# A hybrid MLA and NSA decoder block: a reordered first stage, and q's inverse norm as a factor of the score rows

## The chip, the cores and the metric

The kernel runs on one core of a Trainium2 chip. The metric is the device time of one execution in microseconds, as the median of several runs. PE is the matrix engine, with its weight loads counted apart as PEld; DVE is the vector engine, ACT the scalar engine, POOL the GpSimd engine, and SP the engine whose queue issues nearly all DMAs. [...]

## The reference: what is computed

One decoder block for a sequence of 512 rows of width 1024, in float32. Cut to what matters:

```python
mod = silu(c) @ ada_w + ada_b                       # c: one row; ada_w: 1024 x 6144
sh1, sc1, gt1, sh2, sc2, gt2 = split(mod, 6)
h = rms_norm(x, norm1_gain) * (1 + sc1) + sh1
z = h @ w_in                                        # all projections of both mixers
y_mla = mla_attention(...) @ w_o_mla                # 8 heads, q and k of 96 = 64 + 32 rotary
y_nsa = nsa_attention(...) @ w_o_nsa                # 8 heads of 64: compressed, selected, window
x = x + gt1 * ((sigmoid(g_mla) * y_mla + sigmoid(g_nsa) * y_nsa) @ w_out)
h2 = rms_norm(x, norm2_gain) * (1 + sc2) + sh2
x = x + gt2 * ((silu(h2 @ ffn_w_gate) * (h2 @ ffn_w_up)) @ ffn_w_down)
```

In both mixers q is normed and turned before the scores: `q = rope(rms_norm(q, q_gain))`, `s = q @ k.T * scale`, `p = softmax(s + mask)`. The inverse norm of q is one number for each row and head. Since a rotation keeps a factor of the row, and the score of a row is linear in q, that number may be multiplied in before the product or into the row of scores behind it.

## The kernel before

Tiles have 128 partitions. The 512 rows of x are four tiles (`NT` = 4), the width 1024 is eight slabs (`KD` = 8). Each float32 operand of a large product is split into a high and a low part (`whi` and `wlo` for weights, `hTh` and `hTl` for h), and a product is three matmuls: high by high, low by high, high by low. ACT makes the high part of a weight slab, DVE or POOL the low part. PSUM tiles come from three pools: `mm` with four buffers, `sc` with two, `tp` with two.

**The first stage** (0 to about 70 us) makes h transposed and the first wide product with w_in. `gemm_wide` goes through the eight slabs k; for each, `make_h(k)` needs two columns of the modulation: `mod_column(k)` loads strips of ada_w 128 columns wide (tile `araw`, four row blocks in a DMA, four DMAs for each k), multiplies each row block by its silu(c) with ACT and DVE and adds them up (tile `acc`), two of the blocks added by POOL. For k = 0 some blocks go to PE directly. `mod_sum` adds over the partitions with PE (tile `pm`), then DVE adds the bias and makes `modc`. With `modc`, h of slab k is scaled (`h`, `hTh`, `hTl`), and PE makes 24 matmuls into `wa` and 24 into `wb`. The low parts of these weights are POOL's (`eng_lo=pool`). The 22 small loads (gains, positions, masks, `small_loads`, L502 to L526) are written behind this stage; SP's queue takes them between the strips.

**Preparation of NSA** (to about 170 us): q of NSA (`UQ`) gets its inverse norm `rsq`, gain and rotation; keys (`kd`) and compressed keys follow. **NSA** (170 to 339 us): for each of eight units the scores of a head come out of PE into `pw` and `ps`; DVE adds the mask and takes the row minimum in one instruction (`tensor_tensor_reduce`; scores are negated; the trace calls it CUSTOM_DVE_ANT_0), ACT takes the exponential.

**MLA** (339 to about 575 us): `gemm_tok` makes q in two groups of four heads (`gq`); `use_q` copies it to `qn` (ACT), sums squares (DVE, `msq` from the squares `jq`), applies the rotary gain `g_q` and the rotation (POOL). `norm_q(c)` makes the inverse norm of group c by a chain of small DVE instructions on 128x16 (`rq_i_q`, `rq_h_q`, `rq_m_q`, ending in `rsq`), and multiplies each of the four `qn` by it. `mla_heads` transposes q and k of one head (PE, `pt`) and splits them (`qh`, `ql`, `kh`, `kl`); `mla_scores` makes the scores (`ps`, pool `sc`) and minima; `mla_values` the weighted sum. Between the heads' steps PE is given work from elsewhere: the merge gates (`gp`), and columns of the modulation for later stages (`mods`, DVE's `macc` from strips `raw` of ada_w). `as_filler(norm_q(1))` lays the second group's norm over the steps of head 0, with a quota of 5 steps.

The rest (575 to 914 us) is the merge, w_out and the feed-forward network.

Every instruction is issued through a helper that records it, so all stand at L144 in the trace; DMA issues have their own lines (L253 for weights, L401 for `araw`, L913 for the strips of `mods`). Instructions of an engine run in the order of its queue. A scheduler sets that order from the code and its own estimate of times, so a change also moves instructions elsewhere. Of the DMAs that SP issues a limited number is under way at a time: an issue waits for the landing of an earlier one.

## Time and profile before

| | us |
|---|---|
| median of 3 runs | 918.6 |
| lowest and highest | 915.64, 920.27 |
| the profiled execution | 915.57 |
| its span in the trace | 913.6 |
| PE busy | 850.4 |
| DVE busy | 645.8 |
| ACT busy | 435.6 |
| POOL busy | 202.3 |

The span is the time from the first to the last instruction of the profiled execution; its own time is 2 us longer. The busy time of an engine is an average over stages with different limits, so the rows further down go by stage: how much PE works in a stretch and at what granted clock, and on what it waits. In a timeline row the brackets at the end say how long the engine had been idle and which operation released it.

### The profile page before, as it was taken

To read this page: it belongs to the slowest core of one execution; us is meant where nothing else is said; L and a number is where in the kernel's file an instruction comes from. 1 tells how busy PE (TensorE), PEld (TensorE's weight loads), DVE (VectorE), ACT (ScalarE), POOL (GpSimd) and SP (SyncE) were. 2 spreads that over 40 slices of the span, in tenths; PEclk is the share of its full clock that TensorE was granted. 3 is DMA by queue.
4 is the path that set the end of the run, shared out by engine and by line. 5 is a ranking of instruction groups with operands and counts; after the bars stand their busy time and mean duration, and the time that the engine had idled before them with its cause. 6 is when DMAs were issued, how large, how long until landed. Compare 5 with 4: busy or idle time off the path is not lost.

```text
span 913.6 us, 13079 instructions
## 1 busy us (share of the span) xinstructions
PE 850.4 (93%) x4644; PEld 727.6 (80%) x4644; DVE 645.8 (71%) x1310; ACT 435.6 (48%) x872; POOL 202.3 (22%) x256
## 2 busy tenths in 40 slices
PE   4799999899999996699998989999999999999997
PEld 3689889777787795588776869787899889988986
DVE  6977876778975788557868898866565566455644
ACT  5445655787764733276645344442344224432440
POOL 2422316534332047131228014000000000000000
PEclk9899999999999998699999999999999999999999
DMA  9944545221100743224478770643233413333312
GB/s 306 273 129 121 147 129 146 81 70 53 42 13 35 230 140 114 81 70 157 167 237 304 215 224 25 206 139 97 65 104 115 125 50 104 104 117 91 93 47 92
DMA packets 101732, 115.47 MB, mean 126 GB/s; under 512 B 6036, under 2 KB 74244, under 8 KB 101668
## 3 DMA queue, kind: packets, MB, share of 16 engines
q1 hardware_dynamic: 101508, 114.48, 40.9%
q8 instruction: 36, 0.59, 0.3%
q14 instruction: 28, 0.23, 0.1%
q0 software_dynamic: 64, 0.13, 0.0%
q10 hardware_dynamic: 96, 0.03, 0.0%
HBM read 106.24 MB, written 8.39 MB: 125 GB/s over the span
## 4 chain that ended last, share of the span: by engine, by line
PE 69%; DVE 14%; DMA 9%; issue 3%; ACT 3%; POOL 2%; SPq 1%; DVEq 0%; ACTq 0%; POOLq 0%
PE d L144 13%; PE fu L144 12%; PE gp L144 10%; PE fx L144 6%; PE ga L144 5%; PE fy L144 4%; DMA raw<-in_ada_w_dram 4%; PE pt L144 4%; PE av L144 3%; DMA araw<-in_ada_w_dram 3%; DVE wlo L144 3%; DVE macc L144 2%; PE ps L144 2%; PE wa L144 2%; PE fg L144 2%
## 5 line engine op out<-in xcount | busy, mean ns | idle before, releaser
L144 ACT ACTIVATE whi<-raw 128x1024 fp32r<-128x1024 f32 (+4 forms) x162 | 142.5, 893 | 174.9 <-PE d L144 58.8
L144 DVE TENSOR_TENSOR wlo<-raw,whi 128x1024 fp32r<-128x1024 f32 (+3 forms) x114 | 135.1, 1187 | 71.8 <-ACT whi L144 71.5
L144 POOL TENSOR_TENSOR wlo<-raw,whi 128x512 fp32r<-128x512 f32 (+1 forms) x48 | 66.8, 1410 | 63.5 <-ACT whi L144 59.7
L144 PE MATMUL fu<-h2l,whi 128*128 128x512 f32 (+1 forms) x192 | 71.2, 372 | 0.0
L144 PE MATMUL fu<-h2h,whi 128*128 128x512 f32 (+1 forms) x192 | 70.7, 372 | 0.0
L144 PE MATMUL fu<-h2h,wlo 128*128 128x512 f32 (+1 forms) x192 | 69.9, 373 | 0.0
L144 PE MATMUL d<-whi,mh 128*128 128x512 f32 x176 | 69.8, 398 | 0.0
L144 PE MATMUL d<-wlo,mh 128*128 128x512 f32 x176 | 69.6, 395 | 0.0
L144 PE MATMUL d<-whi,ml 128*128 128x512 f32 x176 | 67.0, 394 | 0.0
L144 ACT ACTIVATE s<-s,mn 128x384 f32<-128x384 f32 (+3 forms) x96 | 52.4, 547 | 27.1 <-DVE mn L144 26.5
L144 DVE TENSOR_TENSOR plo<-pt,phi 128x512 fp32r<-128x512 f32 (+2 forms) x78 | 46.3, 602 | 24.0 <-ACT phi L144 23.6
L144 PE MATMUL gp<-hTh,whi 128*128 128x512 f32 x128 | 55.2, 431 | 0.8 <-ACT qn L144 0.8
L144 ACT ACTIVATE phi<-pt 128x512 fp32r<-128x512 f32 (+2 forms) x78 | 40.1, 526 | 32.0 <-PE pt L144 31.2
L144 PE MATMUL gp<-hTh,wlo 128*128 128x512 f32 x128 | 51.5, 402 | 0.0
L144 PE MATMUL gp<-hTl,whi 128*128 128x512 f32 x128 | 51.3, 401 | 0.0
L144 DVE SCALAR_TENSOR_TENSOR macc<-raw,csil,macc 128x512 f32<-128x512 f32 x45 | 37.2, 832 | 8.1 <-DMA raw<-in_ada_w_dram 7.6
L144 PEld LDWEIGHTS fu<-h2l,whi 128*128 128x128 f32 x192 | 36.2, 188 | 6.1
L144 PEld LDWEIGHTS fu<-h2h,whi 128*128 128x128 f32 x192 | 35.9, 189 | 6.0
L144 PEld LDWEIGHTS fu<-h2h,wlo 128*128 128x128 f32 x192 | 35.6, 189 | 5.6
L144 PEld LDWEIGHTS d<-whi,mh 128*128 128x128 f32 x176 | 33.0, 188 | 8.3 <-issue 0.2
L144 PEld LDWEIGHTS d<-whi,ml 128*128 128x128 f32 x176 | 33.0, 188 | 8.1
L144 PEld LDWEIGHTS d<-wlo,mh 128*128 128x128 f32 x176 | 33.0, 188 | 7.9 <-issue 0.2
(431 smaller groups left out, 2455.3 us busy)
## 6 DMA issues: line engine op xcount, KB each, us to landing
raw<-in_ada_w_dram SPq DMA_DIRECT2D x26, 512.0 KB, 4.5
raw<-in_ffn_w_gate_dram SPq DMA_DIRECT2D x22, 512.0 KB, 3.7
raw<-in_ffn_w_up_dram SPq DMA_DIRECT2D x22, 512.0 KB, 3.8
raw<-in_ffn_w_down_dram SPq DMA_DIRECT2D x22, 512.0 KB, 4.7
araw<-in_ada_w_dram SPq DMA_DIRECT2D x32, 256.0 KB, 5.1
raw<-in_w_in_dram SPq DMA_DIRECT2D x16, 512.0 KB, 3.7
spill<-gs SPq DMA_DIRECT2D x24, 256.0 KB, 2.0
raw<-in_w_in_dram SPq DMA_DIRECT2D x12, 352.0 KB, 3.5
```

What stands on the lines that cost most here:

```text
L144: out = call(*args, **kw)
```

## The change

1. **First stage.** Columns k = 2, 3 and 4, 5 are made in pairs (`PAIRED`) from strips 256 columns wide; the bytes and the number of DMAs stay, each row piece is 1 KB long, not 512 B. Column 0 goes to PE with all its eight blocks, column 1 with four. Of the other columns ACT makes the first block and DVE adds seven; POOL adds nothing. The low parts of w_in in this stage are DVE's.
2. **Small loads.** All 22 are ordered on SP's queue behind the last strip (`late_load`, `follow_dma`).
3. **The row factor.** The multiplications of q by its inverse norm go: four of `UQ` in NSA, eight of `qn` in MLA. The factor becomes the scale of the minima (`scale=rs`, `scale=rsq[...]`) and of the compressed scores. `norm_q` gives one step to its filler quota (1, not 5). The gain `g_q` goes into the rotation tables once (`c2q`, `snq`), and POOL's eight multiplies of `qn` by it go.
4. **Smaller edits.** `kd` is made in one instruction, not two; the rotation of `kpr` in 4 instructions, not 16; the loads of w2 move from POOL's queue to SP's; a DMA scratch area is made smaller.

```diff
-    def mod_column(k):
+    def mod_columns(k, nk, direct):
...
+            raw = ada_strip(r0, nr, k, nk)
...
-                if k == 0 and r < DIRECT:
+                if r < direct:
                     terms.append((src, s))
-                    continue
...
+                elif acc is None:
+                    acc = sp0.tile([P, w], F32, name=f"acc{k}", tag="acc", bufs=2)
                     act.activation(out=acc, in_=src, func=AF.Copy, scale=s)
-                    if r == 1:
-                        pool.tensor_tensor(out=accs[0], in0=accs[0], in1=acc, op=ALU.add)
...
     def make_h(k):
-        pm, terms = mod_column(k)
+        if k not in PAIRED:
+            sums = k, 1, *mod_columns(k, 1, (KD, KD // 2)[k] if k < 2 else 0)
+        elif k % 2 == 0:
+            sums = k, 2, *mod_columns(k, 2, 0)
+        else:
+            sums = None
...
+    def late_load(**kw):
+        follow_dma(sp.dma_start(**kw).ins, ada_last[0])
...
-            sp.dma_start(out=posi[:, t : t + 1], ...)
+            late_load(out=posi[:, t : t + 1], ...)
...
-    run(gemm_wide(hA, w_in, KD, SEG_B, 512, 256, use_q, use_c, hook=make_h, eng_lo=pool))
+    run(gemm_wide(hA, w_in, KD, SEG_B, 512, 256, use_q, use_c, hook=make_h))
...
-            dve.tensor_tensor(out=u, in0=u, in1=rs[:, t, :].unsqueeze(2).broadcast_to([P, 8, 64]), op=ALU.mult)
...
-            for j in range(2):
-                dve.tensor_tensor(out=kd[:, :, j, :], ...)
+            dve.tensor_tensor(out=kd, in0=u.unsqueeze(2).broadcast_to([P, 4, 2, 64]), ...)
...
+            rs = rs_n[:, t, h : h + 1]
-            dve.tensor_tensor(out=cm[:, r, :], ..., op=ALU.add)
+            dve.scalar_tensor_tensor(out=cm[:, r, :], ..., scalar=rs, ..., op0=ALU.mult, op1=ALU.add)
...
-                                     scale=1.0, scalar=3e38, op0=ALU.add, op1=ALU.min, accum_out=mn[:, 0:1])
+                                     scale=rs, scalar=3e38, op0=ALU.add, op1=ALU.min, accum_out=mn[:, 0:1])
...
-                pool.tensor_tensor(out=qn[t][:, hs, 64:96], ..., in1=g_q..., op=ALU.mult)
-                rope(pool, qn[t][:, hs, 64:96], *tables_m(t), mp, f"q{t}")
+                rope(pool, qn[t][:, hs, 64:96], c2q[:, t, :], snq[:, t, 16:32], snq[:, t, 0:16], mp, f"q{t}")
...
-            for u in range(NT):
-                dve.tensor_tensor(out=qn[u][:, hs, :], ..., in1=rsq[:, c, u, :]..., op=ALU.mult)
-                yield
...
-                                     scale=1.0, scalar=3e38, op0=ALU.add, op1=ALU.min, accum_out=mn[:, t : t + 1])
+                                     scale=rsq[:, h // 4, t, h % 4 : h % 4 + 1], scalar=3e38, op0=ALU.add, op1=ALU.min, accum_out=mn[:, t : t + 1])
...
-                pairs.append((as_filler(norm_q(1)), 5))
+                pairs.append((as_filler(norm_q(1)), 1))
```

How the queues stand, at three places. **First place:** DVE's queue in the first stage, from h of k = 0 to `modc` of k = 1. Before:

```order
30 L144 TENSOR_SCALAR h_220<-px_192,modc 128x512
31 L144 SCALAR_TENSOR_TENSOR acc_0_251<-araw,csil,acc_0_251 128x256
32 L144 TENSOR_TENSOR hTl_143<-h_220,hTh_142 128x512
33 L144 SCALAR_TENSOR_TENSOR acc_0_251<-araw,csil,acc_0_251 128x256 x5
34 L144 SCALAR_TENSOR_TENSOR acc_0_316<-araw,csil,acc_0_316 128x256 x6
35 L144 TENSOR_TENSOR modc<-pm,cols 128x2
36 L144 SCALAR_TENSOR_TENSOR modc<-modc,cols 128x1
```

And now, where acc_323 is the sum of the pair k = 2, 3:

```order
30 L144 TENSOR_SCALAR h_224<-px_193,modc 128x512
31 L144 SCALAR_TENSOR_TENSOR acc_323<-araw,csil,acc_323 128x512
32 L144 TENSOR_TENSOR hTl_143<-h_224,hTh_142 128x512
33 L144 SCALAR_TENSOR_TENSOR acc_323<-araw,csil,acc_323 128x512
34 L144 TENSOR_TENSOR wlo<-raw,whi 128x768
35 L144 SCALAR_TENSOR_TENSOR acc_323<-araw,csil,acc_323 128x512
36 L144 TENSOR_TENSOR wlo<-raw,whi 128x768
37 L144 SCALAR_TENSOR_TENSOR acc_323<-araw,csil,acc_323 128x512 x3
38 L144 TENSOR_TENSOR modc<-pm,cols 128x1 x2
39 L144 SCALAR_TENSOR_TENSOR acc_323<-araw,csil,acc_323 128x512
40 L144 SCALAR_TENSOR_TENSOR modc<-modc,cols 128x1
```

Before, eleven sums of columns 1 and 2 (256 wide) stood between `hTl` of k = 0 and `modc` of k = 1; now six sums of the pair (512 wide) and two `wlo` stand between h of k = 0 and `modc` of k = 1.

**Second place:** DVE's queue ahead of `modc` of k = 4. Before, with `CAST posf` behind k = 1's work:

```order
41 L144 TENSOR_TENSOR hTl_145<-h_277,hTh_144 128x512
42 L144 SCALAR_TENSOR_TENSOR acc_0_377<-araw,csil,acc_0_377 128x256 x2
43 L144 CAST posf<-posi 128x5
44 L144 SCALAR_TENSOR_TENSOR acc_0_377<-araw,csil,acc_0_377 128x256
45 L144 SCALAR_TENSOR_TENSOR acc_0_438<-araw,csil,acc_0_438 128x256
```

And now, where `modc` is that of k = 4 and 5, and acc_597 the sum of k = 7:

```order
53 L144 SCALAR_TENSOR_TENSOR acc_537<-araw,csil,acc_537 128x256 x5
54 L144 TENSOR_TENSOR wlo<-raw,whi 128x768
55 L144 SCALAR_TENSOR_TENSOR acc_537<-araw,csil,acc_537 128x256 x2
56 L144 CAST posf<-posi 128x5
57 L144 TENSOR_TENSOR modc<-pm,cols 128x2 x2
58 L144 SCALAR_TENSOR_TENSOR modc<-modc,cols 128x2
59 L144 SCALAR_TENSOR_TENSOR acc_597<-araw,csil,acc_597 128x256 x2
60 L144 TENSOR_SCALAR g_q<-g_q 128x32
61 L144 TENSOR_SCALAR g_n<-g_n 128x64
62 L144 SCALAR_TENSOR_TENSOR acc_597<-araw,csil,acc_597 128x256
63 L144 TENSOR_TENSOR hTl_151<-h_459,hTh_150 128x512
```

The cast of the positions and the two instructions on `g_q` and `g_n`, all fed by small loads, now stand around the `modc` of the second pair and ahead of `hTl` of k = 4.

**Third place:** DVE's queue at the start of the MLA heads, from the end of the second group's chain to the minima of head 0 (the instruction called ISA here). Before:

```order
674 L144 SCALAR_TENSOR_TENSOR rsq<-rq_m_q_4269,rq_i_q_4267 128x16
675 L144 TENSOR_TENSOR qn_3540<-qn_3540,rsq 128x384
676 L144 TENSOR_TENSOR qn_3541<-qn_3541,rsq 128x384
677 L144 SCALAR_TENSOR_TENSOR macc<-raw,csil,macc 128x512 x2
678 L144 TENSOR_TENSOR qn_3542<-qn_3542,rsq 128x384
679 L144 ISA s_4192,mn<-ps,mask 128x128
680 L144 ISA mn 128x1
681 L144 ISA s_4211,mn<-ps,mask 128x256
682 L144 ISA mn 128x1
683 L144 TENSOR_TENSOR qn_3543<-qn_3543,rsq 128x384
684 L144 SCALAR_TENSOR_TENSOR macc<-raw,csil,macc 128x512
685 L144 ISA s_4221,mn<-ps,mask 128x384
```

And now:

```order
659 L144 SCALAR_TENSOR_TENSOR kl<-pt,cols_701,kh 96x512
660 L144 SCALAR_TENSOR_TENSOR rsq<-rq_m_q_4281,rq_i_q_4279 128x16
661 L144 SCALAR_TENSOR_TENSOR macc<-raw,csil,macc 128x512 x2
662 L144 ISA s_4136,mn<-ps,mask,rsq 128x128
663 L144 ISA mn 128x1
664 L144 ISA s_4155,mn<-ps,mask,rsq 128x256
665 L144 ISA mn 128x1
666 L144 ISA s_4165,mn<-ps,mask,rsq 128x384
667 L144 ISA mn 128x1
668 L144 ISA s_4175,mn<-ps,mask,rsq 128x512
669 L144 ISA mn 128x1
```

The four `qn` multiplies are gone, and both `macc` that stood between the minima stand elsewhere; the minima have `rsq` as an operand.

## Rows read from the trace of the kernel before

**Rows 1.** The page, busy microseconds of each engine, share of the span, instructions.
```profile
PE 850.4 (93%) x4644; PEld 727.6 (80%) x4644; DVE 645.8 (71%) x1310; ACT 435.6 (48%) x872; POOL 202.3 (22%) x256
```

**Rows 2.** Windows: stretch, its length, each engine's busy time, granted clock, DMA share, GB/s.
```profile
18.00:48.00 30.00, 24.20 (x120) 20.68 (x121) 27.85 (x43) 13.61 (x23) 15.04 (x10) 0.89 0.98 281
...
170.00:339.00 169.00, 165.12 (x846) 133.38 (x846) 130.47 (x391) 114.08 (x306) 55.49 (x76) 1.00 0.26 80
339.00:384.00 45.00, 29.92 (x120) 24.25 (x119) 36.05 (x76) 17.11 (x40) 24.94 (x41) 0.74 0.35 111
```

**Rows 3.** Timeline of PE, first stage: start, length, engine, line, operation, count, idle before.
```profile
10.35 2.29 PE L144 MATMUL pm<-csil,araw 128*128 128x1 f32 x10 [0.26 <-DMA araw<-in_ada_w_dram]
...
18.60 0.79 PE L144 MATMUL wa<-whi,hTh 128*128 128x512 f32 x1
...
31.25 1.12 PE L144 MATMUL px<-ident,x 128*128 128x128 f32 x4 [2.40 <-DVE modc L144]
...
34.34 0.78 PE L144 MATMUL wa<-whi,hTh 128*128 128x512 f32 x1
...
50.90 0.50 PE L144 MATMUL wa<-whi,hTh 128*128 128x512 f32 x1 [0.61 <-ACT hTh L144]
```

**Rows 4.** Timeline of ACT at the end of the first stage.
```profile
69.59 2.07 ACT L144 ACTIVATE UQ<-wa 128x512 f32<-128x512 f32 x4 [2.29 <-PE wa L144]
```

**Rows 5.** Timeline of DVE, first stage.
```profile
20.30 10.82 DVE L144 SCALAR_TENSOR_TENSOR acc<-araw,csil,acc 128x256 f32<-128x256 f32 x11
```

**Rows 6.** Groups by line and form, 0 to 72 us: count, busy, mean ns, idle.
```profile
L144 DVE SCALAR_TENSOR_TENSOR acc<-araw,csil,acc 128x256 f32<-128x256 f32 x46 | 33.9, 741 | 1.2 <-DMA araw<-in_ada_w_dram 0.4
...
L144 POOL TENSOR_TENSOR wlo<-raw,whi 128x768 fp32r<-128x768 f32 x8 | 15.1, 1898 | 25.1 <-ACT whi L144 21.5 <-DVE hTl L144 3.4 <-DMA vec<-in_mla_kv_a_gain_dram 0.2
...
L144 DVE TENSOR_TENSOR wlo<-raw,whi 128x536 fp32r<-128x536 f32 x3 | 2.1, 711 | 0.0
```

**Rows 7.** Timeline of SP's queue, start of the strips of ada_w.
```profile
8.33 3.02 SPq L401 DMA_DIRECT2D araw<-in_ada_w_dram  x4
```

**Rows 8.** Timeline of PE, start of the MLA heads.
```profile
349.39 0.28 PE L144 MATMUL pt<-ident,qn 128*96 128x128 f32 x1 [3.44 <-DVE qn L144]
...
353.05 0.79 PE L144 MATMUL gp<-hTh,whi 128*128 128x512 f32 x1 [0.79 <-ACT qn L144]
...
369.14 0.69 PE L144 MATMUL ps<-kh,qh 96*128 96x384 f32 x1 [6.80 <-DVE mn L144]
...
374.35 0.45 PE L144 MATMUL ps<-kh,qh 96*128 96x128 f32 x1 [2.60 <-DVE mn L144]
...
378.58 1.70 PE L144 MATMUL pt<-ident,s 128*128 128x128 f32 x7
```

**Rows 9.** Timeline of DVE, start of the MLA heads.
```profile
347.26 1.19 DVE L144 SCALAR_TENSOR_TENSOR rsq<-rq_m_q,rq_i_q 128x16 f32<-128x16 f32 x1
348.55 2.35 DVE L144 TENSOR_TENSOR qn<-qn,rsq 128x384 f32<-128x384 f32 x4
350.83 0.74 DVE L144 SCALAR_TENSOR_TENSOR macc<-raw,csil,macc 128x512 f32<-128x512 f32 x1
...
362.70 2.10 DVE L144 TENSOR_TENSOR qn<-qn,rsq 128x384 f32<-128x384 f32 x2
364.73 2.60 DVE L144 SCALAR_TENSOR_TENSOR macc<-raw,csil,macc 128x512 f32<-128x512 f32 x2
...
368.80 0.28 DVE L144 CUSTOM_DVE_ANT_0 s<-ps,mask 128x128 f32<-128x128 f32 x1
...
372.98 0.75 DVE L144 SCALAR_TENSOR_TENSOR macc<-raw,csil,macc 128x512 f32<-128x512 f32 x1 [3.07 <-DMA raw<-in_ada_w_dram]
...
374.79 0.68 DVE L144 CUSTOM_DVE_ANT_0 s<-ps,mask 128x512 f32<-128x512 f32 x1
```

**Rows 10.** Timeline of POOL, start of the MLA heads.
```profile
343.42 4.99 POOL L144 TENSOR_TENSOR wlo<-raw,whi 128x512 fp32r<-128x512 f32 x4
```

**Rows 11.** Timeline of ACT, start of the MLA heads.
```profile
352.12 0.49 ACT L144 ACTIVATE jq<-gq 128x384 f32<-128x384 f32 x1 [6.06 <-DVE msq L144]
```

More of the change, by code (lines that the diff above doesn't have):

```diff
@@ L391, in hybrid_block @@
     modc = cst.tile([P, 6, KD], F32, name="modc")
-    def mod_column(k):
-        pm = tp.tile([P, S], F32, name="pm", tag="tp")
-        terms, accs = [], []
-        soft = -1 if k == 0 else 1
-        for r0 in range(0, KD, 4):
-            raw = sp0.tile([P, 1024], F32, name="araw", tag="araw", bufs=6)
-            rv = raw.rearrange("p (r s n) -> p r s n", r=4, s=2)
-            for i in range(2):
-                sp.dma_start(out=rv[:, :, i, :], in_=rows(ada, r0 * P, 4, i * D + k * P, P))
-            for r in range(r0, r0 + 4):
+    ada_last = [None]
@@ new lines, in hybrid_block, with ada_strip @@
+    PAIRED = (2, 3, 4, 5)
+    def ada_strip(r0, nr, k, nk):
+        raw = sp0.tile([P, 1024], F32, name="araw", tag="araw", bufs=6)
+        rv = raw.rearrange("p (r s n) -> p r s n", r=nr, s=2)
+        for i in range(2):
+            ada_last[0] = sp.dma_start(out=rv[:, :, i, :], in_=rows(ada, r0 * P, nr, i * D + k * P, nk * P)).ins
+        return raw
+    def mod_columns(k, nk, direct):
+        pm = tp.tile([P, S], F32, name="pm", tag="tp")
+        terms, acc = [], None
+        nr = 4 // nk
+        w = 2 * nk * P
+        for r0 in range(0, KD, nr):
+            raw = ada_strip(r0, nr, k, nk)
+            for r in range(r0, r0 + nr):
@@ L421, in mod_column, with mod_sum @@
         return pm, terms
[L423 to L431 removed]
+    def mod_sum(k, nk, pm, terms):
+        n = 2 * nk
+        for j, (v, s) in enumerate(terms):
+            for i in range(n):
+                pe.matmul(pm[:, i : i + 1], v[:, i * P : (i + 1) * P], s, start=(j == 0 and i == 0), stop=(j == len(terms) - 1), skip_group_check=True)
+        c = V_AB + k
+        for i in range(2):
+            dve.tensor_tensor(out=modc[:, i, k : k + nk], in0=pm[:, i * nk : (i + 1) * nk],
+                              in1=cols[:, c + i * KD : c + i * KD + nk], op=ALU.add)
+        v = modc[:, 1, k : k + nk]
+        dve.scalar_tensor_tensor(out=v, in0=v, scalar=1.0, in1=cols[:, V_N1 + k : V_N1 + k + nk], op0=ALU.add, op1=ALU.mult)
@@ L446, in make_h @@
             scale_x(3 * P, D)
-        if k > 0:
-            mod_sum(k, pm, terms, (0, n))
-        dve.scalar_tensor_tensor(out=modc[:, 1, k : k + 1], in0=modc[:, 1, k : k + 1], scalar=1.0,
-                                 in1=cols[:, V_N1 + k : V_N1 + k + 1], op0=ALU.add, op1=ALU.mult)
+        if k > 0 and sums:
+            mod_sum(*sums)
         h = sp0.tile([P, S], F32, name=f"h{k}", tag="h", bufs=2)
```

89 lines of the change are left out of this document (43 added, 46 removed).

## Prediction, made before the changed kernel ran

> **What bounds the kernel now.** I read the page's busy times first: TensorE works 850.4 us of a span of 913.6 [rows 1]. So only time in which PE waits, or runs at a lowered clock, can be won. The windows by stage say where that is: between 18 and 48 us PE works 24.2 of 30 us at a granted clock of 0.89, and between 339 and 384 us, where the MLA heads begin, 29.9 of 45 us at 0.74; in the 169 us of NSA it works 165.1 [rows 2]. The first and second of these stretches lie in the change's way; in NSA an engine made lighter can give almost nothing. Third, the timelines of PE and of the engine that it waits for, in these two stretches.
>
> In the first stage k=0 starts at 18.60, k=1 only at 34.34, after PE has waited for DVE's `modc` (2.40 us before the transposes at 31.25); k=4 starts at 50.90 and the wide product is over at 69.59, when ACT copies `UQ` out [rows 3, 4]. DVE does eleven sums in a row from 20.30 to 31.12 before k=1's `modc`; the mean of all 46 is 0.74 us [rows 5, 6], while POOL's `wlo` run beside them.
>
> At the MLA start PE waits 3.44 us for DVE's `qn`, another 0.79 for ACT's `qn` (a PSUM buffer), 6.80 and 2.60 us for DVE's row minima [rows 8]. DVE shows why: the last step of the inverse norm ends at 348.45, stretched to 1.19 us beside POOL's four `wlo` (343.42 to 348.41); then come four `qn` multiplies; later two more (2.10 us), two `macc` (2.60), one more multiply and only then the first minimum at 368.80; the third minimum stands behind a `macc` that waits 3.07 us for a DMA [rows 9, 10]. ACT's square at 352.12 had waited 6.06 us for the DVE reduce in DVE's queue [rows 11].
>
> **The change part by part.** All sums are made on the profiled execution, 915.57 us, which is the fastest of the runs shown; the median is 918.6, so 3.0 us are added at the end.
>
> *First stage.* Start: k=0's sum is now all on PE, 32 instructions for 16. Ten took 2.29 us [rows 3], so the 16 more cost 3.7 us, of which some are hidden, because before PE waited here for the norm of x. I let k=0 start 1.1 us later, 19.7. DVE then has, ahead of k=1's `modc`, six pieces of the pair's sum and two `wlo` of w_in (first order excerpt). Their price: a 512-wide sum 0.74 with POOL idle [rows 9]; a 768-wide `wlo` on DVE isn't in the trace, the nearest rows are 0.71 us for 536 columns on DVE and 1.90 for 768 on POOL [rows 6]; I take 0.95, by the DVE row. That is 4.4 + 1.9 us, some 8 with `h` and its low part, so 27.7, if the strips are there. The strips of k=0, k=1 and six of the pair's eight with six slabs of w_in are 6.0 MB from 8.33 on [rows 7]; at the 281 GB/s of rows 2 the last is there at about 30. `modc`, `h` and its high part follow; before, k=1 came 3.1 us after the wait for `modc` had ended at 31.25, with transposes of two columns in between at half the clock; I take 2.3: k=1 at 32.3, 2 us early. From there k=2 and k=3 have their sums early, and PE runs through three slabs, at the 4.7 us that one took on the mean from 50.90 to 69.59, to about 46.5.
>
> Then the moved loads count. All 22 small loads now stand behind the last strip on SP, and DVE's queue has `CAST posf<-posi` directly ahead of the `modc` of k=4 and 5 (second excerpt). The strips and w_in are 11.5 MB; at 281 GB/s from 8.33 they are through at 49, and earlier without the small loads between them, which that rate holds; I take 47.5 for them and 48 for the positions. k=4 then starts at about 50 (49 to 52) where PE could have started at 46.5: the gain is down to 1 us. Four slabs took 18.7 us before (50.90 to 69.59); they now need no sums of their own in k=5 and DVE is lighter, but `g_n`, the last of the small loads, stands ahead of k=4's low part. I take 17.7 us: the stage ends at 67.7, **2 us early**, with bounds from 5 early (the loads land with the strips) to 3 late (k=4 at 54 to 55).
>
> On the wider strips I count nothing, because at k=4 the small loads decide. [...]
>
> *Preparation of NSA, 96 to 170 us.* Four `UQ` multiplies on DVE go, four `kd` multiplies become two-in-one, the `kpr` ropes are batched; PE's transposes of `UQ` move ahead of a product. POOL's ropes, ready before them in the trace, decide whether that waits. I take **0.5 us lost**, between 2.5 won and 2.5 lost. Where the eight w2 and `kd` instructions go, PE is busy and the cost is nothing; without that cover it would be their own few tenths.
>
> *NSA.* The minima (64) and the 32 compressed scores now take the row factor as a scale. No row shows this minimum with a pointer for its scale. The nearest rows are the minimum itself, 0.68 us for 128x512 with a constant, and a sum of the same size with a pointer, 0.74 [rows 9]: so 0 to +0.06 each. DVE has 38.5 us to spare in this stage [rows 2] and takes up at most 6 of them. I take **0**.
>
> *MLA start.* (a) PE's transposes of `qn` now need only POOL's ropes, which end where the four `wlo` begin, 343.42 [rows 10]; they start when PE is free, 349.39 less 3.44 = 345.95. (b) The product `gp` still waits for ACT's `qn`, which waits for the DVE reduce behind the chain. Out of its way go four multiplies (2.35 us), into it comes one more `macc` (0.74) [rows 9, 11], so `gp` starts at 353.05 - 1.6 = 351.4: the first gap moves behind the transposes instead of closing, and gives 1.6 us. (c) Up to the second chain all hangs on `ql`, `kl` of head 1 and so on PE, 1.6 us early: the chain that ended just before 362.70 ends at 361.0, two `macc` at 0.74 follow, and the first minimum stands at 362.5 in place of 368.80 (third excerpt): 6.3 us won. (d) The other minima now follow each other with no multiply and no DMA between. Before, head 1's first score came 5.55 us after the first minimum (374.35 less 368.80); now two scores and two minima (0.68 for the wider) lie between, some 2 us: 364.5, so 9.8 us won. (e) From there to the transposes of the weights it was 4.2 us (374.35 to 378.58 [rows 8]) at a lowered clock; with some of it at full clock about 3.3: 367.8 instead of 378.6, 10.8 won. (f) The lowered clock lasted to 384 us (0.74 as the mean of 45 us [rows 2]); I credit 1.2 us for what of this tail runs at full clock. Sum: **12 us won**. Bounds: 14.5, if the gap in (b) closes too and the clock stays up, and 6, if only (c) holds and DVE's queue meets the DMA again in front of the minima. Dropping POOL's `g_q` steps hides behind (b) and costs or gives nothing by itself.
>
> *The rest.* Nothing of the change lies behind 384 us but the 24 MLA minima of the later heads, priced as in NSA.
>
> Sum: -2 + 0.5 + 0 - 12 = -13.5; 902 for an execution like the profiled one, 905 for the median.
>
> **The rivals.** *A, the late loads cost more than the strips give:* `posi` and `g_n` land at 52 to 54, PE stands still at k=4, and the first stage ends 3 us late. For it: 22 more issues in one row on a queue whose DMAs fill the engines until then [rows 2]; against it: they are tiny. The MLA part stays: 905 + 5 = 910.
> *B, the MLA stall moves instead of going:* the two `macc` ahead of the first minimum wait for their strip, as the one at 372.98 does now (3.07 us), and the clock falls again at the gap in (b). Then 6 us are won there: 911; with A as well 916.
> *C, slower than before:* the minimum with a pointer scale costs much more. DVE's 38.5 us to spare over 96 instructions are 0.40 us each; from there on DVE is NSA's bound, and at 0.55 more each the 13.5 us are used up. If it cost a whole second pass, 0.68, NSA would grow by 96 x 0.28 = 27 us: 932. Against it stands the sum with a pointer at 0.74.
> *D, the path isn't moved:* the order of work shifts elsewhere (the preparation stage waits for POOL's ropes) and eats 8 to 10 us: 914.
>
> **How the numbers follow.** The forecast 0.58 (900 to 908), A 0.18, B 0.12, C 0.03, D 0.09. I predict 905. The best bounds together (5 + 2.5 + 14.5) give 897; the worst ends of the forecast's terms with A or B reach 914 to 916. The range 896 to 913 leaves out C, about half of D and the overlap of A and B. A measurement of this kernel can tell about 0.5% (4.6 us) from no change. Faster by more than that: the forecast, nearly all of A, most of B and half of D, 0.86; within: 0.10; slower: 0.04.
>
> **What would show it.** In the profile of the changed kernel: k=1's first product near 32.5, k=4's near 50 behind `CAST`; `UQ` copied out at about 67.7; DVE sums with a mean of 0.49 (256 wide) and 0.74 (512 wide) with POOL idle; the `qn` transposes directly behind `gq`, a gap of 3 to 4 us behind them, the first minimum about 6 us after head 1's `ql`, no gap over 2.5 us between the scores of heads 0 and 1, and minima no longer than before. The prediction is wrong if the minima are longer by more than 0.1 us, if PE stands still for over 4 us at k=4, or if a new gap of over 4 us stands in front of the scores of head 0 or in the preparation of NSA.

## The result, and the profile after

The changed kernel takes **907.33 us** (median of 4 runs, 906.09 to 909.51), the kernel before, run beside it, 917.22 (915.64 to 920.27). The ratio is 0.9902 with a 95% interval of 0.9881 to 0.9923: 9.9 us faster. Its profiled execution took 906.09 us with a span of 904.0, against 915.57 and 913.6.

The page of the changed kernel, busy time of PE (it answers to [rows 1]):

```profile
PE 855.2 (95%) x4676; PEld 731.4 (81%) x4676; DVE 636.0 (70%) x1288; ACT 432.4 (48%) x863; POOL 176.3 (20%) x222
```

PE has 32 instructions more and works 4.8 us more in a span 9.6 us shorter: what went is time in which PE stood still. Its windows, with two of [rows 2] and two more (columns as there; the clock records of both kernels' traces hold 1.00 and 0.50 alone, so a figure between them is the mean of a stretch):

```profile
18.00:48.00 30.00, 26.88 (x149) 23.09 (x148) 23.92 (x49) 12.72 (x19) 0.00 (x0) 0.94 0.93 290
164.00:180.00 16.00, 13.57 (x67) 10.79 (x68) 11.78 (x59) 12.21 (x47) 5.31 (x9) 0.89 0.21 59
339.00:384.00 45.00, 37.45 (x173) 31.61 (x171) 31.30 (x74) 21.19 (x51) 21.20 (x31) 0.81 0.32 100
360.00:376.00 16.00, 12.76 (x39) 10.33 (x40) 10.39 (x29) 7.39 (x21) 4.52 (x4) 0.57 0.26 82
```

And the same two added stretches of the kernel before:

```profile
164.00:180.00 16.00, 13.23 (x75) 10.49 (x75) 12.43 (x67) 14.17 (x50) 7.47 (x22) 1.00 0.24 65
360.00:376.00 16.00, 6.30 (x26) 4.73 (x25) 11.05 (x24) 5.08 (x12) 6.04 (x8) 0.74 0.27 87
```

In the first stage PE's work rose by 2.7 us of 30, in the MLA start by 7.5 of 45. Two rows speak against the change: the granted clock at the start of NSA (164 to 180 us) fell from 1.00 to 0.89, and between 360 and 376 us PE works twice as long as before, but at 0.57. At a clock of 0.50 the 128x512 matmuls of `gp` followed each other every 0.43 us (373.4 to 375.1 us), at 1.00 every 0.23 (178.1 to 180 us).

The timeline of PE in the first stage answers to [rows 3]:

```profile
19.62 0.79 PE L144 MATMUL wa<-whi,hTh 128*128 128x512 f32 x1
...
31.79 1.05 PE L144 MATMUL pm<-ones,acc 128*128 128x1 f32 x8 [1.41 <-ACT h L144]
32.70 0.48 PE L144 MATMUL wa<-whi,hTh 128*128 128x512 f32 x1
...
48.16 0.63 PE L144 MATMUL px<-ident,x 128*128 128x128 f32 x4 [0.86 <-DVE modc L144]
...
49.73 0.50 PE L144 MATMUL wa<-whi,hTh 128*128 128x512 f32 x1
```

Column k = 0 starts 1.0 us later than before, k = 1 1.6 earlier, k = 4 1.2 earlier. The end is ACT's copy of `UQ`, 1.55 us earlier than in [rows 4]:

```profile
68.04 2.06 ACT L144 ACTIVATE UQ<-wa 128x512 f32<-128x512 f32 x4 [2.27 <-PE wa L144]
```

What holds k = 4 stands in DVE's timeline and in SP's:

```profile
47.71 0.17 DVE L144 CAST posf<-posi 128x5 f32<-128x5 int32 x1 [2.74 <-DMA vec<-in_mla_q_gain_dram]
```

```profile
36.99 3.00 SPq L404 DMA_DIRECT2D araw<-in_ada_w_dram  x4
...
43.24 3.02 SPq L510 DMA_DIRECT2D posi<-in_positions_dram  x6
```

And the load rate, last number of the windows around it:

```profile
40.00:43.00 3.00, 3.00 (x20) 2.64 (x19) 2.61 (x6) 0.78 (x1) 0.00 (x0) 1.00 0.97 251
...
44.00:48.00 4.00, 3.29 (x21) 2.76 (x20) 1.23 (x6) 0.51 (x1) 0.00 (x0) 1.00 0.21 40
```

The strips are issued by 40 us, their bytes move until about 43 us, and by the trace the last of them lands at 44.77. Between 44 and 48 us the DMA engines are four fifths idle while SP hands out the small loads one behind the other, and DVE waits 2.74 us for the positions (the row names a small load issued next to them). The first of the small loads aren't free of the strips either; SP's queue waits between 40 and 48 us:

```profile
SPq L510 <- DMA araw<-in_ada_w_dram: 1.8, 4, 0.6
```

Four times, 1.8 us in all, an issue of a small load waits for the landing of a strip, the last time for the one at 44.77, which frees the third of the six `posi`.

The MLA start on PE, which answers to [rows 8]:

```profile
345.70 0.60 PE L144 MATMUL pt<-ident,qn 128*96 128x128 f32 x4
...
350.43 0.50 PE L144 MATMUL gp<-hTh,whi 128*128 128x512 f32 x1 [3.69 <-ACT qn L144]
...
362.23 0.69 PE L144 MATMUL ps<-kh,qh 96*128 96x384 f32 x1 [2.85 <-DVE mn L144]
...
364.64 0.31 PE L144 MATMUL ps<-kh,qh 96*128 96x128 f32 x1
...
368.74 1.70 PE L144 MATMUL pt<-ident,s 128*128 128x128 f32 x7
```

The four waits of [rows 8] (3.44, 0.79, 6.80, 2.60 us) have become two, of 3.69 and 2.85. On DVE, answering to [rows 9], the chain of the inverse norm and the first minimum:

```profile
341.56 0.17 DVE L144 SCALAR_TENSOR_TENSOR rq_i_q<-rq_m_q,rq_i_q 128x16 f32<-128x16 f32 x1
341.77 1.31 DVE L144 TENSOR_TENSOR rq_m_q<-rq_i_q,rq_h_q 128x16 f32<-128x16 f32 x1
343.11 1.22 DVE L144 TENSOR_TENSOR rq_m_q<-rq_m_q,rq_i_q 128x16 f32<-128x16 f32 x1
344.36 1.21 DVE L144 SCALAR_TENSOR_TENSOR rq_i_q<-rq_m_q,rq_i_q 128x16 f32<-128x16 f32 x1
345.61 1.20 DVE L144 TENSOR_TENSOR rq_m_q<-rq_i_q,rq_h_q 128x16 f32<-128x16 f32 x1
346.84 0.24 DVE L144 TENSOR_TENSOR rq_m_q<-rq_m_q,rq_i_q 128x16 f32<-128x16 f32 x1
...
359.50 2.41 DVE L144 SCALAR_TENSOR_TENSOR macc<-raw,csil,macc 128x512 f32<-128x512 f32 x2
361.83 0.34 DVE L144 CUSTOM_DVE_ANT_0 s<-ps,mask,rsq 128x128 f32<-128x128 f32 x1
```

Beside it POOL, as in [rows 10], and ACT, as in [rows 11]:

```profile
341.75 5.03 POOL L144 TENSOR_TENSOR wlo<-raw,whi 128x512 fp32r<-128x512 f32 x4 [1.36 <-ACT whi L144]
...
359.91 3.14 POOL L144 TENSOR_TENSOR wlo<-raw,whi 128x512 fp32r<-128x512 f32 x2 [1.95 <-ACT whi L144]
```

```profile
349.50 0.49 ACT L144 ACTIVATE jq<-gq 128x384 f32<-128x384 f32 x1 [3.53 <-DVE msq L144]
```

The first gap of PE is read backwards through these rows: `gp` waits for a PSUM buffer that ACT's `qn` empties; `qn` stands behind ACT's square `jq`, which waits for one of its two buffers; the buffer is freed by DVE's `msq`, and that stands behind two `macc` (1.66 us) and the chain, of which four steps on 16 columns took 1.2 to 1.3 us each in place of 0.17, just while POOL's `wlo` ran.

The price of the pointer: minima and compressed scores by form, before

```profile
L144 DVE CUSTOM_DVE_ANT_0 s<-ps,mask 128x512 f32<-128x512 f32 x16 | 11.0, 684 | 5.0 <-PE ps L144 2.7 <-POOL wlo L144 2.1
...
L144 DVE TENSOR_TENSOR cm<-pw,consts 128x32 f32<-128x32 f32 x32 | 5.9, 184 | 8.9 <-PE pw L144 8.8
```

and after:

```profile
L144 DVE SCALAR_TENSOR_TENSOR cm<-pw,rs_n,consts 128x32 f32<-128x32 f32 x32 | 7.8, 243 | 5.9 <-PE pw L144 5.8
...
L144 DVE CUSTOM_DVE_ANT_0 s<-ps,mask,rs_n 128x512 f32<-128x512 f32 x8 | 5.9, 740 | 0.6 <-PE ps L144 0.6
```

Each costs 0.06 us more (684 to 740 ns, 184 to 243 ns), at 128, 256 and 384 columns too (286 to 345, 419 to 481 and 549 to 610 ns).

### The profile page after: what moved, and what is told of

The parts are those of the page before. It is cut to its first block, busy times and chain, and to the rows that moved or that the text cites. A ratio compares the mean times of both kernels' runs of the same rounds, so it can differ in the third digit from the quotient of the medians.

```text
span 904.0 us, 13055 instructions
## 1 busy us (share of the span) xinstructions
PE 855.2 (95%) x4676; PEld 731.4 (81%) x4676; DVE 636.0 (70%) x1288; ACT 432.4 (48%) x863; POOL 176.3 (20%) x222
## 4 chain that ended last, share of the span: by engine, by line
PE 73%; DVE 13%; DMA 7%; ACT 2%; issue 2%; SPq 1%; POOL 1%; DVEq 0%; POOLq 0%; ACTq 0%
PE d L144 14%; PE fu L144 13%; PE gp L144 9%; PE fx L144 6%; PE ga L144 5%; PE fy L144 4%; PE pt L144 4%; PE av L144 3%; DMA raw<-in_ada_w_dram 3%; PE fg L144 3%; PE wa L144 2%; DVE macc L144 2%; PE gwo L144 2%; DVE wlo L144 2%; PE ps L144 2%
## 5 line engine op out<-in xcount | busy, mean ns | idle before, releaser
L144 DVE TENSOR_TENSOR wlo<-raw,whi 128x1024 fp32r<-128x1024 f32 (+3 forms) x122 | 144.0, 1184 | 73.5 <-ACT whi L144 73.1
L144 ACT ACTIVATE s<-s,mn 128x384 f32<-128x384 f32 (+2 forms) x96 | 52.5, 548 | 23.0 <-DVE mn L144 22.3
L144 POOL TENSOR_TENSOR wlo<-raw,whi 128x512 fp32r<-128x512 f32 x40 | 52.3, 1329 | 44.4 <-ACT whi L144 44.4
```

The costliest lines, as they stand in the source:

```text
L144: out = call(*args, **kw)
```

## The experiments

All ratios are to the kernel before, run beside each. The table takes one profiled execution of each kernel and tells how many us PE gained on the kernel before in each stretch; its borders are the same PE instructions in all: a `wa` product just behind the first stage (71.42 us before), the first `cm` transpose of NSA (173.25), a `gq` product 1.2 us ahead of the last (344.40), the weights' transposes of head 0 (378.58), the last product (908.25). Negative is lost.

| kernel | first stage | preparation | NSA and q's product | MLA start | rest | sum | ratio, interval |
|---|---|---|---|---|---|---|---|
| changed kernel | 1.6 | 1.3 | -2.8 | 9.8 | -0.3 | 9.5 | 0.9902 [0.9881, 0.9923] |
| e1 stage alone | 0.7 | 1.5 | 0.4 | 0.3 | 0.0 | 2.8 | 0.9994 [0.9979, 1.0010] |
| e2 row factor alone | -0.3 | 1.1 | -0.5 | 10.0 | -0.9 | 9.6 | 0.9944 [0.9914, 0.9974] |
| e3 NSA factor undone | 0.2 | 0.1 | 0.6 | 10.5 | -1.2 | 10.1 | 0.9882 [0.9854, 0.9910] |
| e4 four buffers | 1.6 | 1.3 | -0.3 | 13.3 | 2.5 | 18.3 | 0.9825 [0.9796, 0.9854] |
| e5 four buffers, before | -0.5 | 1.4 | -1.5 | 3.6 | 1.4 | 4.4 | 0.9954 [0.9935, 0.9974] |
| e6 chain later | 1.2 | -1.2 | -1.2 | 13.6 | 1.2 | 13.6 | 0.9834 [0.9805, 0.9862] |
| e7 early loads | -1.8 | 1.1 | 0.5 | 10.6 | -1.4 | 9.1 | 0.9918 [0.9890, 0.9946] |
| e8 low parts on POOL | 0.5 | -1.2 | -0.5 | 8.5 | -0.2 | 7.1 | 0.9928 [0.9882, 0.9974] |
| e9 own strip | -0.6 | -0.2 | -9.6 | 18.9 | 3.1 | 11.7 | 0.9861 [0.9844, 0.9877] |
| e10 the same, NSA factor undone | 1.2 | 0.1 | -8.1 | 19.2 | -2.3 | 10.1 | 0.9848 [0.9819, 0.9878] |
| e11 narrow strips | -2.8 | 1.8 | -1.6 | 8.6 | -0.9 | 5.0 | 0.9934 [0.9908, 0.9959] |
| e12 strips behind the weights | 0.8 | 1.3 | -3.1 | 13.8 | -0.7 | 12.1 | 0.9873 [0.9841, 0.9905] |

How far one execution carries is seen in the table itself: the changed kernel and e3, e4, e6, e9, e10 and e12 have the same first stage in their code and gain between -0.6 and 1.6 us there; in the preparation the changed kernel, e4, e6, e9 and e12 have PE's work in the same order and gain between -1.2 and 1.3. A difference under some 2.5 us isn't told apart by two rows of it. The profiled execution is also the fastest one of the changed kernel, e1, e2, e4 and e7, so their sums flatter them.

### Which part gives what: e1, e2

The two parts were made alone, in the kernel before: in **e1** the first stage with its late loads, in **e2** the row factor with the smaller edits.

```diff
+    PAIRED = (2, 3, 4, 5)
...
+        follow_dma(sp.dma_start(**kw).ins, ada_last[0])
```

> The kernel before with the new first stage and the late small loads alone; q's inverse norm is multiplied in as before. Theory: the trace of the changed kernel has its wide product over 1.55 us earlier than the kernel before, and PE bounds what follows, so 1 to 2.5 us faster than before at the end (ratio 0.997 to 0.999), with k=4 again held by the cast of the positions at about 48 to 50 us and the UQ copies at 68.0. Rival: the lead is eaten by the waits in the preparation of NSA (96 to 170 us), and the time is that of before (ratio 0.9995 to 1.001).

e1 took 915.48 us beside 915.99. Its profile shows 2.8 us won, but that execution is its fastest (912.57); ten runs say 0.5 us, between 0.9 us lost and 1.9 won. That is nearer to the rival; the theory's 1 to 2.5 us aren't excluded up to 1.9. The rival's reason isn't seen, since the profiled execution keeps its lead (2.2 us at the start of NSA, 2.8 at the end). What the stage is worth by itself stays under what can be measured here.

```diff
+            rs = rs_n[:, t, h : h + 1]
...
-                pairs.append((as_filler(norm_q(1)), 5))
+                pairs.append((as_filler(norm_q(1)), 1))
```

> The kernel before with the row factor and the small edits (kd, kpr, w2, tables) alone; the first stage and the small loads as before. Theory: the parts add up, and nearly all comes from the start of the MLA heads: 7 to 9 us faster than before (ratio 0.990 to 0.993), with a gap of 3 to 4 us behind the qn transposes and one of 2 to 4 us in front of the third score, and the granted clock at 0.5 for about 8 us there. Rival: most of the gain needs both parts, since only the time at which NSA begins sets where the clock falls: under 6 us.

e2 took 909.57 us beside 915.99, 6.4 less (2.4 to 7.9 by the interval), between the theory's 7 to 9 and the rival's 6; its ten runs lie far apart, from 905.75 to 916.31. Its profile, of the fastest of them, wins 10.0 us in the MLA start, as the changed kernel's. There its PE timeline has the same two gaps:

```profile
350.99 0.79 PE L144 MATMUL gp<-hTh,whi 128*128 128x512 f32 x1 [4.57 <-ACT qn L144]
...
362.74 0.45 PE L144 MATMUL ps<-kh,qh 96*128 96x384 f32 x1 [2.85 <-DVE mn L144]
```

So most of the gain comes with the row factor and the smaller edits, in the MLA start; no run parts these two. The two runs' ratios multiply to 0.9938, against 0.9902 for both parts together, which is no more than the three intervals allow.

### The gap behind the transposes: e4, e5

Theory: ACT's square waits for a buffer, so four buffers close PE's first gap.

```diff
-                jq = mp.tile([P, 4, MQK], F32, name="jq", tag="jq", bufs=2)
+                jq = mp.tile([P, 4, MQK], F32, name="jq", tag="jqq", bufs=4)
```

> The changed kernel with four buffers in place of two for the squares of q (jq), so that ACT needn't wait for DVE's reduces before it copies qn out of PSUM. Theory: the gap of 3.69 us behind the qn transposes is that wait; gp starts near 347 in place of 350.43, the clock stays up there, and the kernel gains 2 to 4 us on the changed one (903 to 905.5). Rival: the gain is given back in front of the third and fourth minimum, where this order again has a macc that can wait for its DMA strip (3.07 us in the kernel before): within 1 us of the changed kernel.

The edit also parts the buffers: so far q's squares shared two with k's, here they have four of their own. The wait of 3.53 us above names `msq`, the sum over q's own squares, so the number is the likelier cause; the parting alone was not run. e4 took **900.43 us** (897.00 to 901.36), 6.9 less than the changed kernel and the fastest of all; the two intervals don't overlap. `gp` follows the transposes at once:

```profile
344.34 0.50 PE L144 MATMUL gp<-hTh,whi 128*128 128x512 f32 x1
...
353.03 1.09 PE L144 MATMUL pt<-ident,kn 128*96 128x128 f32 x4 [2.94 <-DVE ql L144]
```

The 3.69 us gap is gone, a new one of 2.94 us stands at the next thing that DVE owes. Not all that its profile wins is the buffers': of the 8.8 us over the changed kernel 3.5 lie in the MLA start and 2.8 behind it, but 2.5 in NSA, where the code of both is the same. In **e5** the kernel before got the four buffers, with the two small edits that make room for them.

```diff
-        pool.dma_start(out=w2, ...)
+        sp.dma_start(out=w2, ...)
...
+                jq = mp.tile([P, 4, MQK], F32, name="jq", tag="jqq", bufs=4)
...
+    nc = bacc.Bacc(..., dynamic_dma_scratch_size=2048)
```

> The kernel before (with its qn multiplies) with four buffers for the squares of q; to make room the w2 loads go through SP's queue and the DMA scratch area is small, as in the changed kernel. Theory: the two things stand one behind the other on DVE, so without the row factor the buffers give less: PE's first wait (3.44 us for qn) stays, gp starts 2 to 3 us earlier, and the first minimum still stands behind the qn multiplies; 2 to 4 us faster than before (ratio 0.9955 to 0.998). Rival: the buffers are what counts and the row factor hardly adds to them: 6 us or more faster than before.

It took 912.90 us beside 916.60: 3.7 less, as the theory had it. Its waits for `qn` (3.15 us) and for the minima (5.07 and 2.56 us) stay, as the wait for ACT's `qn` stays in e2: each edit clears its own wait and leaves the other. In the table's MLA column the two add up (3.6 and 10.0 us, beside 13.3 in e4). By the medians the buffers alone give 3.7 us, the row factor 6.4 and the first stage 0.5, together 10.6 where e4 has 15.6; that the parts help each other isn't shown by this, since e2's runs lie so far apart.

### What DVE owes next: e6, e9, e10, e12

**e6** adds to e4 that the second group's chain is ordered behind the last DVE instruction of the head step ahead of it, so that `ql` doesn't wait for it.

```diff
+            if c == 1:
+                dve.gate = dve.last
```

> The changed kernel with four buffers for the squares, and the second group's chain of small DVE instructions ordered behind the last DVE instruction written before it, so that ql and kl of heads 0 and 1 and head 0's minima stand ahead of it. Theory: in the run with four buffers PE waits 2.94 us for ql, which stands behind this chain (some of its steps take 1.2 us beside POOL); with the chain behind, ql comes 3 us earlier, no gap over 1 us is left before the scores of head 0, the clock stays up, and the kernel gains 2 to 4 us on that run (896.5 to 898.5 where that had 900.4). Rival: the minima then meet the macc and its DMA strip again, as in the kernel before, and PE waits there: no gain, 899.5 to 902.

It took 901.41 us, no better than e4. The wait for `ql` is gone, and the rival came true, on DVE first and then on PE:

```profile
360.48 0.75 DVE L144 SCALAR_TENSOR_TENSOR macc<-raw,csil,macc 128x512 f32<-128x512 f32 x1 [4.06 <-DMA raw<-in_ada_w_dram]
```

```profile
361.92 0.44 PE L144 MATMUL ps<-kh,qh 96*128 96x128 f32 x1 [4.35 <-DVE mn L144]
```

A sum that waits for a strip stands between two minima, as in [rows 9] (3.07 us there). **e9** adds to e6 a buffer of their own for the strips, so that they don't wait for a weight buffer.

```diff
+    strip_src.update(pool=mcp, bufs=1)
```

> The changed kernel with four buffers for q's squares, the second group's norm chain written behind the last DVE instruction of the head step ahead of it, and a strip buffer of its own for the column sums macc (they share no weight buffer any more). Theory (after the buffer and the chain, the wait of macc for a DMA in DVE's queue is the last long wait of the MLA start): neither the 2.94 us gap of PE behind the kn transposes nor the 4.35 us gap behind macc is there, head 0's minima follow each other, and the kernel takes 896 to 899 us. Rival (the strips come as late as before, or another wait takes the place): a gap of over 2.5 us stays between 350 and 365 us and the time is 900 us or more.

It took 904.13 us. The MLA start is as the theory has it, with no gap over 0.5 us and the clock at 1.00 throughout, but the time was lost before, where PE waits for the weights of `gk`:

```profile
313.41 1.20 PE L144 MATMUL gk<-whi,cTh 128*128 128x512 f32 x4 [2.68 <-ACT whi L144]
...
339.00:384.00 45.00, 43.43 (x239) 37.57 (x239) 39.89 (x98) 27.25 (x65) 28.92 (x44) 1.00 0.36 116
```

In SP's queue a strip now stands ahead of these weights and waits for the one buffer. Beside these waits the granted clock was lower there: 0.93 in the mean from 296 to 345 us, where the changed kernel has 1.00. **e10** is e9 with the NSA row factor undone, by the same edit as e3 below, where both are read.

```diff
-            rs = rs_n[:, t, h : h + 1]
...
+            dve.tensor_tensor(out=u, in0=u, in1=rs[:, t, :].unsqueeze(2).broadcast_to([P, 8, 64]), op=ALU.mult)
```

> As e9_own_strip, but q of NSA is multiplied by its inverse norm again (four more multiplies, the 96 minima and compressed scores with a constant for their scale). Theory (the pointer costs 0.06 us on an engine with time to spare, and the preparation gains about 1 us from the four multiplies that go): 0 to 2 us slower than e9_own_strip. Rival (the longer minima cost the NSA stage, which lost 2 us of its lead in the changed kernel): 1 to 3 us faster than e9_own_strip.

**e12** is e9 with a pair of buffers for the strips, and that only from q's product on, so that the weights go first.

```diff
-    strip_src.update(pool=mcp, bufs=1)
...
+        strip_src.update(pool=mcp, bufs=2)
         for c in range(2):
             with_side(gemm_tok(sel_ct(0), a["mla_w_q_b"][0], 6, ...
```

> As e9_own_strip, but the strips of the column sums go into a buffer pair of their own only from the start of q's product on (before it they take weight buffers as in the changed kernel), so in SP's queue they stand behind the weights of the key and q products. Theory (what e9_own_strip lost was PE's waits of 2.68 and 2.29 us for the weights of gk behind strips that waited for the one buffer, and what it won in the MLA start was real): gk starts as early as in the changed kernel, the MLA start runs without a gap over 2 us as in e9_own_strip, the lead at the end is 20 to 24 us over the kernel before in the profile, and the time is 893 to 898 us. Rival (the wait moves once more, or the loss of e9_own_strip between 300 and 335 us was the clock alone): a gap of over 2 us between 300 and 365 us, or the lowered clock there, and 899 us or more.

It took 903.61 us: the rival again. The long wait for the weights is gone (the last `gq` is 9.3 us earlier than in e9, the clock there 1.00), but so is the clean MLA start:

```profile
356.40 1.09 PE L144 MATMUL pt<-ident,kn 128*96 128x128 f32 x4 [2.75 <-DVE ql L144]
```

Now DVE's `ql` stands behind four `kn` multiplies (3.87 us) and four `msq`. So e9's 18.9 us in the MLA start look in good part like a loan: PE came to it 10.4 us later than in the kernel before, and DVE, POOL and the loads had that time to get ahead. None of the three beat e4. From the changed kernel to e12 a wait of 2.7 to 4.4 us went from the squares to `ql`, to a strip, to the weights of `gk` and back to `ql`.

### The start of NSA: e3, e10

The changed kernel is 2.9 us ahead at 173 us and 0.9 at 195. Theory: the pointers' 0.06 us are paid there. In **e3** q of NSA is multiplied by its inverse norm again.

```diff
+            dve.tensor_tensor(out=u, in0=u, in1=rs[:, t, :].unsqueeze(2).broadcast_to([P, 8, 64]), op=ALU.mult)
...
-                                     scale=rs, scalar=3e38, op0=ALU.add, op1=ALU.min, accum_out=mn[:, 0:1])
+                                     scale=1.0, scalar=3e38, op0=ALU.add, op1=ALU.min, accum_out=mn[:, 0:1])
```

> The changed kernel with the row factor of NSA undone (UQ multiplied by its inverse norm on DVE, minima with the constant 1.0, compressed scores by an addition); MLA's row factor and all else stay. Theory: the lead that the changed kernel loses between 160 and 300 us (from 2.5 to 0.9 us) comes from the pointer scale, 0.06 us on each of 96 DVE instructions, and from the lowered clock at 168 to 176 us that its waits on the minima bring; undone, the lead stays: 1 to 2 us faster than the changed kernel (905 to 906.5). Rival: the waits at NSA's start come from the order of the preparation, not from the minima: the same time, 907 to 908.5, with the clock still lowered near 170 us.

e3 took 904.88 us, e10 904.17 beside 904.13 for e9. In the profiles e3 loses the preparation's gain (0.1 for 1.3) and keeps NSA (0.6 for -2.8); by the medians e3 is 2.4 us faster than the changed kernel and e10 as fast as e9, and the intervals overlap in both pairs, so what the NSA half of the row factor is worth stays open. That the pointers alone don't make the loss is shown by e4, which has the same 96 and loses 0.3:

```profile
164.00:180.00 16.00, 13.57 (x73) 10.89 (x74) 13.17 (x61) 12.22 (x48) 5.83 (x10) 1.00 0.19 57
```

From the end of the first stage to 170 us e4 and the changed kernel run alike, to 0.1 us; in this execution the granted clock stayed at 1.00, in the other it fell to 0.89, and with that the difference of 1.6 us at 195 came up. Over all profiles the clock fell in this stretch in 6 of the 9 executions with the factor in NSA (to between 0.68 and 0.89) and in none of 5 without. PE's waits for DVE's minima there are a little longer with it (0.73, 1.36, 0.57 and 0.57 us in the changed kernel; 0.88, 0.37 and 0.37 before). One execution of each makes that likely, not shown.

### The first stage: e7, e8, e11

**e7** takes the late order of the small loads away.

```diff
-        follow_dma(sp.dma_start(**kw).ins, ada_last[0])
+        sp.dma_start(**kw)
```

> The changed kernel with the 22 small loads left to the scheduler's order, between the strips, as in the kernel before. Theory of the prediction: the late loads hold k=4 (the trace of the changed kernel shows PE waiting 0.86 us at 48.2 and 0.89 us for its low part at 53.2); with early loads the cast no longer waits, but the strips land later for the slots that the loads take, so k=1 starts 0.5 to 2 us later and k=4 0 to 2 us earlier: within 1.5 us of the changed kernel at the end of the stage, within 2 us in the whole time. Rival: the late loads are what makes the first stage faster at all; with early loads the stage ends later than in the kernel before: over 2 us slower than the changed kernel.

e7 took 908.83 us, the changed kernel 907.33: not told apart, as the theory has it for the time. In the profile the theory fails: k = 1 starts 3.0 us and k = 4 5.0 us later than in the changed kernel, and the stage ends 3.3 us later, 1.8 later than in the kernel before, as the rival has it. PE waits 4.39 us ahead of k = 1:

```profile
33.97 1.87 PE L144 MATMUL pm<-ones,acc 128*128 128x1 f32 x8 [4.39 <-ACT h L144]
```

**e8** gives the low parts of w_in back to POOL.

```diff
-    run(gemm_wide(hA, w_in, KD, SEG_B, 512, 256, use_q, use_c, hook=make_h))
+    run(gemm_wide(hA, w_in, KD, SEG_B, 512, 256, use_q, use_c, hook=make_h, eng_lo=pool))
```

> The changed kernel with the low parts of w_in in the first stage on POOL again. Theory: DVE's sums are stretched beside POOL (0.74 us in place of 0.49 for 256 columns in the kernel before), 21 sums of 0.49 or 0.74 and more cost DVE what the eight slabs of 0.95 save it, and k=1 starts 1 to 3 us later: the stage ends 0 to 2 us later than the changed kernel's. Rival: POOL was free and the sums wait for strips anyway: no change, or the stage ends earlier by up to 1 us.

It took 908.18 us (905.0 to 915.4), not told apart either. But its groups by form give a price (0 to 72 us; the number behind the comma is the mean in ns):

```profile
L144 DVE SCALAR_TENSOR_TENSOR acc<-araw,csil,acc 128x256 f32<-128x256 f32 x17 | 12.6, 742 | 6.5 <-ACT acc L144 6.2
```

The same group in the changed kernel, with POOL idle:

```profile
L144 DVE SCALAR_TENSOR_TENSOR acc<-araw,csil,acc 128x256 f32<-128x256 f32 x17 | 8.2, 481 | 1.9 <-ACT acc L144 1.6
```

The same 17 sums take 742 ns in the mean with the low parts on POOL, as the 741 of [rows 6], and 481 without. The chain's steps above point the same way: 0.17 us each without POOL's `wlo` and 1.2 beside it, about as long as one `wlo` (1.26 us, 5.03 for four). Why DVE is slower there no run shows.

**e11** makes all strips 128 columns wide.

```diff
-    PAIRED = (2, 3, 4, 5)
+    PAIRED = ()
```

> The changed kernel with strips of ada_w 128 columns wide throughout (row pieces of 512 B, no pairs of columns). [...] Rival (the width of a piece plays no part): the same rate within 1%, k = 4 within 0.5 us, the same time.

It took 910.37 us (903.79 to 916.14), 3 more than the changed kernel with intervals that overlap. In the profile the rival didn't come true. k = 4 starts at 46.56 us, 3.2 earlier than in the changed kernel, since its `modc`, no longer shared with k = 5, stands ahead of the cast in DVE's order. But the small loads go out 2.9 us later, the positions reach DVE 3.1 us later, and now PE waits there for the next `modc`, ahead of k = 5:

```profile
42.95 0.84 SPq L510 DMA_DIRECT2D vec<-in_norm_gain_dram  x1
```

```profile
50.83 0.17 DVE L144 CAST posf<-posi 128x5 f32<-128x5 int32 x1 [4.32 <-DMA posi<-in_positions_dram]
```

```profile
56.13 1.12 PE L144 MATMUL px<-ident,x 128*128 128x128 f32 x4 [4.78 <-DVE modc L144]
```

k = 5 starts at 58.20 us (55.55 in the changed kernel), and the stage ends 4.3 us later. The load rate while the strips flow, between 20 and 36 us, of e11:

```profile
20.00:36.00 16.00, 15.64 (x90) 13.79 (x91) 14.82 (x34) 7.96 (x13) 0.00 (x0) 1.00 1.11 331
```

and of the changed kernel, with the first of its small loads:

```profile
20.00:36.00 16.00, 14.59 (x77) 12.60 (x77) 13.69 (x25) 6.83 (x10) 0.00 (x0) 0.89 1.08 363
```

```profile
40.08 0.40 SPq L510 DMA_DIRECT2D vec<-in_norm_gain_dram  x1
```

With wide pieces the rate was 10% higher (363 against 331 GB/s). Between 18 and 48 us e11 has 298 GB/s and the changed kernel 290; but the changed kernel's strips are through at 43 us and its DMA engines stand nearly idle behind them (a share of 0.21 from 44 to 48 us), so that mean hides the difference. By the packet records of the trace, 8 to 50 us, the changed kernel's 4096 packets of 1 KB took 49.7 ns each in the mean and its 6305 of 512 B 31.5 (30.9 in the kernel before): a fifth less per byte. So with the wide strips the first of the small loads that stand behind them goes out 2.9 us earlier (40.08 for 42.95). What that is worth in the whole time isn't told apart by these runs.

## Why the prediction held, and where it was off

The forecast was 905, the result 907.33, inside the range, and faster by more than 0.5%. The profile won 9.5 us where 13.5 were worked out: 1.6 for 2 in the first stage, 1.3 for -0.5 in the preparation, -2.8 for 0 in NSA with q's product, 9.8 for 12 in the MLA start, and -0.3 behind it. That the median came within 2.3 us of the forecast is in part luck: 1.4 us come from the kernel before, whose median was 917.2 with one run more, not 918.6.

**First stage: right, by two errors that cancelled.** Its times came as worked out: k = 0 at 19.62 (19.7), k = 1 at 32.70 (32.3), `CAST` at 47.71 (48), k = 4 at 49.73 (about 50), the end at 68.04 (67.7). But the last strip landed at 44.8, not at 47.5: I took the rate of 281 GB/s from the kernel before, and it was 363 between 20 and 36 us. And from there the positions took 2.9 us, not 0.5, because the small loads follow each other on a nearly idle DMA, at 40 GB/s. That the time of the positions came out is luck. "On the wider strips I count nothing, because at k=4 the small loads decide" was wrong in its reason: the small loads stand behind the strips on one queue, and with narrow strips (e11) they went out 2.9 us later. Rival A (3 us late) didn't come, though the order of the loads did decide k = 4. And e1 puts the part at 0.5 us (at most 1.9), so what the 2 us are worth in the time can't be told.

**Preparation: not told apart.** 0.5 lost was said, 1.3 won was seen to 173 us, inside the bounds of 2.5; but with PE's work in the same order e6 lost 1.2 there, so even the sign is open.

**NSA at 0: a term without its first microseconds.** The price of the pointer was right, at its upper bound (+0.06 us each), and over the whole stage DVE had room for it. What was left out was the start of the stage, where DVE isn't ahead yet and PE waits four times for its minima; there the clock fell (0.89 from 164 to 180 us), and NSA with q's product gave back 2.8 us. I had argued from the mean of 169 us ("38.5 us to spare"), which hides its first ten. How much of it is the change's stays open: with the same code e4 lost 0.3 and e12 3.1.

**MLA start: each step hit but the last two.** The times can be compared with the forecast's because the lead from the earlier stages was down to 0.1 us here. (a) 345.70 for 345.95; (b) `gp` at 350.43 for 351.4, with the gap of 3.69 us where "3 to 4" was said (4.1 in e3, e7, e8 and e11, whose code here is the same); (c) the first minimum at 361.83 for 362.5; (d) head 1's first score at 364.64 for 364.5. The chain of (c) ended 1.4 us earlier than worked out, at 359.57, and the two `macc` behind it took 2.41 us where 1.48 was priced: POOL's `wlo` ran beside them, which [rows 10] showed for the first chain and I didn't carry over. That is also why a gap of 2.85 us stands where "none over 2.5" was forecast. (e) and (f) failed: the clock's credit. From (d) to the weights' transposes it took 4.1 us again, not 3.3, since the clock stood at 0.57 from 360 to 376; what followed won another 1.4 us to 395.56 and had lost 2.7 by 460.89. So 9.8 us instead of 12.

**Rivals.** B was the nearest: the gap moved, and the clock fell behind it. But the gap moved to where (b) had put it, the two `macc` didn't wait for their strip, and 9.8 us were won where B had 6. C is excluded (0.06 and not 0.55 us each). D didn't come: the preparation gained.

**What I passed over** is that the pair of buffers of `jq` was behind the gap in (b). I followed it to the chain in DVE's queue and counted what the change takes out of that queue, without asking why ACT needs DVE at all there. e4 shows that a gain of 6.9 us by the medians lay one line away.

## To carry to other kernels

Follow a wait back to the resource, not only to the engine: if an engine waits for another that merely frees a buffer, try more buffers and not the shorter queue alone; here they gave 3.7 us by themselves and 6.9 on top of the change. Price small DVE instructions by what POOL does beside them (here 0.17 us alone, 1.2 to 1.3 beside `wlo`), and give no credit for a clock that might rise (here it stood at 0.57 from 360 to 376 us). A rate over a window says little when the transfers end inside it. A stage's mean slack says nothing on its first microseconds; and a stage that looks clean behind a new stall may have been paid for by that stall.
